# Eight rows, three projections: older rows' products placed ahead of each new row on TensorE

## The chip, the cores and the metric

The kernel runs on one core of one Trainium2 chip. The metric is the device time of one execution in microseconds (us). A core has five engines that run beside each other and wait for each other by semaphores: TensorE (in the profile PE for matmuls, PEld for the weight loads that go with them), VectorE (DVE), ScalarE (ACT), GpSimd (POOL) and SyncE (SP, which here issues most DMAs). Each engine works through its own list of instructions in a fixed order.

## The reference

The reference is a decoder trunk of two layers over 512 tokens of width 1024. The part that matters here is the entry of the first layer: the input is normalised, multiplied by a gain, and projected.

```python
def rms_norm(x, g):
    xf = x.astype(jnp.float32)
    y = xf * lax.rsqrt(jnp.mean(xf * xf, axis=-1, keepdims=True) + EPS)
    return (y * g.astype(jnp.float32)).astype(x.dtype)
...
h = rms_norm(x, ln_mix[layer])
mkv = mem_n @ w_mem_kv[layer]
...
proj = h @ w_in
...
b_logit = proj[..., o2:o2 + GDN_HEADS].astype(jnp.float32)
a_logit = proj[..., o2 + GDN_HEADS:o2 + 2 * GDN_HEADS].astype(jnp.float32)
```

`proj` holds, per token, queries, keys and values of six heads (128 wide each), a gate `z`, twelve columns of logits for the gates `a` and `b`, and queries into 256 memory tokens. `mkv` gives keys and values of these memory tokens, for both layers. After the entry come a convolution over time, the gated delta rule, an output projection, two feed-forward blocks and a second layer with sliding-window attention; the change touches none of them.

## The kernel before, in words

Everything is kept transposed: the width of 1024 lies in eight rows of 128 partitions, the 512 tokens lie along the free dimension. "Row k" below is one such slab of 128 x 512. Matmuls are done in a split form: a number is written as a high part (rounded) and a low part (the rest), and a product of two such numbers takes three matmuls, high by high, high weight by low activation, low weight by high activation. That is `mm3` (L196): three matmuls of 128 x 512, in the profile `pj<-h,whi`, `pj<-l,whi` and `pj<-h,wlo`. A weight block of 128 x 1024 is split by `weight` (L182): ScalarE copies it into `whi`, VectorE subtracts to get `wlo`. Three such pairs exist at a time, so a fourth block waits until the first is used up.

`mem_and_norm` (L294) computes the keys and values of the memory tokens for both layers, and the norm of x. For the second layer's, `values` (L371) accumulates two tiles, each 128 x 256, in two PSUM banks with the tag `pj`; ScalarE later scales them out into `kt` (L387), which frees these banks. PSUM is divided at L251: three banks with tag `pj`, two with `g`, three with `sc`. A bank is given to a new tile once the last reader of its old tile is done.

`first_rows` (L429) is the place of the change. It opens four accumulations of 128 x 512: `self.ab` (a `sc` bank), the twelve gate columns; and `begun[0]`, `begun[1]`, `begun[2]` (three `pj` banks), the first three key projections, heads 0, 1 and 2. It then loops over k. For k below eight it prepares row k: VectorE multiplies x by gain and norm (L447, `x<-x,gains,xr`), ScalarE makes the high part (L448, `h<-x`), VectorE the low part (`l<-x,h`); then come two matmuls of the gate columns (L450 and L451, `sc<-h,wabs` and `sc<-l,wabs`). At k = 1 and k = 3 the weights of the second and third projection are split. At k = 4 the tiles `kt` are evicted: `next(keys)` and `next(values)`; in `values` the copy is placed behind the ScalarE copy of row 4 by an ordering edge (`after = self.copied`, L384 and L388). Last in each turn come the products: projection 0 takes row k, projection 1 row k - 2, projection 2 row k - 5 (`trail = (0, 2, 5)`).

What order the instructions have on each engine is settled when the program is built: a planner takes, by its own estimates of time, the instruction that is ready and stands earliest in the program text. `nosync` (L116) adds an edge that fixes that one instruction stands behind another on the same engine; on the chip it costs no semaphore. The finished order on each engine is then fixed, and the engine waits at an instruction whose input, or whose bank, isn't ready.

After the loop, `gates` (L482, called at k = 8) copies `ab` out, sorts it with eight small matmuls, and computes the gates in a long chain over ScalarE, VectorE, TensorE and a DMA. `gdn` (L541) goes on: the three begun projections are convolved (`conv_tile`, L531), put through Silu and transposed, while TensorE works at the next projections.

Of the kernel before, what the change touches and what calls it, by code (L numbers as in the profile page):

```python
# [21 lines left out]
KD = D // P  # L22
# [64 lines left out]
class Builder:  # L87
# [108 lines left out]
    def mm3(self, ps, w, k, act, start, stop, more=False):  # L196

        (wh, wl), (ah, al) = w, act
        s = slice(k * P, (k + 1) * P)
        self.mm(ps, wh[:, s], ah, start, False, more)  # L200
        self.mm(ps, wh[:, s], al, False, False, more)
        self.last = self.mm(ps, wl[:, s], ah, False, stop, more)

# [225 lines left out]
    def first_rows(self, ep, x, xr, keys, values):  # L429

        nc, w = self.nc, []
        self.h = []
        self.ab = self.bank("sc")
        self.begun = [self.bank("pj") for _ in range(3)]

        def product(h, k):
            if 0 <= k < KD:
                self.mm3(self.begun[h], w[h], k, self.h[k], k == 0, k == KD - 1)


        trail = (0, 2, 5)
        w.append(self.weight(self.a["win"][H]))
        for k in range(KD + trail[-1]):
            if k < KD:
                self.h.append(self.pair(self.apool))
                xk = x[:, k, :]
                self.stt(xk, xk, self.gain(G_MIX[0], k), xr, ALU.mult, ALU.mult)  # L447
                self.split(xk, *self.h[k])  # L448
                hi, lo = self.h[k]
                self.mm(self.ab, self.wab[:, k, :], hi, k == 0, False)  # L450
                self.mm(self.ab, self.wab[:, k, :], lo, False, k == KD - 1)  # L451
                if k == 4:
                    next(keys)
                    next(values)
                if k in (1, 3):
                    w.append(self.weight(self.a["win"][H + len(w)], after=(self.copied, self.low)))
            elif k == KD:
                self.gates(ep)
            for h, n in enumerate(trail):
                product(h, k - n)  # L460

    def memory_columns(self, mr, mc, after):

# [1053 lines left out]
```

## Time and profile before

| | |
|---|---|
| median of 3 runs | 1143.69 us (1141.78, 1143.69, 1144.18) |
| the profiled execution's own time | 1142.63 us |
| its span, first to last instruction | 1140.8 us |
| TensorE busy with matmuls | 1128.5 us, 99% of the span |
| weight loads | 991.3 us, 87% |
| VectorE, ScalarE, GpSimd | 831.0, 632.0 and 86.6 us |
| mean granted TensorE clock | 0.998 of full speed |

In a timeline, a row gives the start and the duration in us, the engine, the line of the kernel (a helper's line, so L146 is every matmul and L140 nearly every ScalarE copy), the operation, the tile written and those read, the shape, how many such instructions follow each other, and, in brackets, idle time of the engine ahead of it and what ended that. Matmuls are pipelined: a row of 0.39 us starts every 0.23 us, so the time that a matmul takes is read from start to start. In a table of windows, a row gives the busy time of each engine in a stretch, with the number of instructions, then the granted clock, the share of the DMA engines and GB/s.

### The profile page before, as it was taken

To read this page: it belongs to the slowest core of one execution; us is meant where nothing else is said; L and a number is where in the kernel's file an instruction comes from. 1 tells how busy PE (TensorE), PEld (TensorE's weight loads), DVE (VectorE), ACT (ScalarE), POOL (GpSimd) and SP (SyncE) were. 2 spreads that over 40 slices of the span, in tenths; PEclk is the share of its full clock that TensorE was granted. 3 is DMA by queue.
4 is the path that set the end of the run, shared out by engine and by line. 5 is a ranking of instruction groups with operands and counts; after the bars stand their busy time and mean duration, and the time that the engine had idled before them with its cause. 6 is when DMAs were issued, how large, how long until landed. Compare 5 with 4: busy or idle time off the path is not lost. (4 is left out here: it accounts for less than half of the span.)

```text
span 1140.8 us, 19304 instructions
## 1 busy us (share of the span) xinstructions
PE 1128.5 (99%) x7337; PEld 991.3 (87%) x7337; DVE 831.0 (73%) x1543; ACT 632.0 (55%) x1267; POOL 86.6 (8%) x99
## 2 busy tenths in 40 slices
PE   9999999999999999999999999999999999999996
PEld 9888778887899988899988787788999988999886
DVE  7664976577888975588955877839989544889554
ACT  8588664566566632366643555956566322666433
POOL 0230000000111001011000000000111000111000
PEclk9999999999999999999999999999999999999999
DMA  8344242234667536378533321116677533776232
GB/s 311 117 143 148 93 130 85 84 120 148 180 148 195 140 107 175 109 169 201 128 92 98 131 73 38 56 42 199 151 190 180 141 97 104 182 187 146 85 94 86
DMA packets 72560, 151.15 MB, mean 132 GB/s; under 512 B 16860, under 2 KB 18932, under 8 KB 72468
## 3 DMA queue, kind: packets, MB, share of 16 engines
q1 hardware_dynamic: 61060, 129.21, 35.9%
q0 software_dynamic: 11136, 20.45, 11.0%
q8 instruction: 57, 0.93, 0.3%
q14 instruction: 35, 0.29, 0.1%
q10 hardware_dynamic: 272, 0.26, 0.1%
HBM read 142.94 MB, written 6.96 MB: 131 GB/s over the span
## 5 line engine op out<-in xcount | busy, mean ns | idle before, releaser
L140 ACT ACTIVATE whi<-wraw 128x512 fp32r<-128x512 f32 (+3 forms) x318 | 236.0, 749 | 248.5 <-PE pj L146 163.5
L153 DVE TENSOR_TENSOR wlo<-wraw,whi 128x512 fp32r<-128x512 f32 (+3 forms) x318 | 264.6, 842 | 94.2 <-ACT whi L140 88.6
L146 PE MATMUL pj<-h,whi 128*128 128x512 f32 (+1 forms) x652 | 256.4, 395 | 0.0
L146 PE MATMUL pj<-l,whi 128*128 128x512 f32 (+1 forms) x652 | 254.6, 391 | 0.0
L146 PE MATMUL pj<-h,wlo 128*128 128x512 f32 (+1 forms) x652 | 254.2, 390 | 0.0
L146 PE MATMUL g<-T,whi 128*128 128x256 f32 x1216 | 218.6, 280 | 0.6 <-ACT fs L140 0.6
L146 PEld LDWEIGHTS g<-T,whi 128*128 128x128 f32 x1216 | 186.0, 188 | 2.0 <-DVE fu L156 1.2
L146 PE MATMUL g<-T,wlo 128*128 128x256 f32 x608 | 170.1, 280 | 0.0
L146 PEld LDWEIGHTS pj<-h,whi 128*128 128x128 f32 x652 | 122.5, 188 | 27.5 <-issue 3.4
L146 PE MATMUL g<-h,wlo 128*128 128x256 f32 (+1 forms) x500 | 146.0, 292 | 0.0
L146 PE MATMUL g<-l,whi 128*128 128x256 f32 (+1 forms) x500 | 146.0, 292 | 0.0
L146 PE MATMUL g<-h,whi 128*128 128x256 f32 (+1 forms) x500 | 145.6, 291 | 0.0
L146 PEld LDWEIGHTS pj<-h,wlo 128*128 128x128 f32 x652 | 122.5, 188 | 25.1 <-issue 0.9
L146 PEld LDWEIGHTS pj<-l,whi 128*128 128x128 f32 x652 | 122.7, 188 | 24.4 <-issue 0.6
L146 PEld LDWEIGHTS g<-T,wlo 128*128 128x128 f32 x608 | 114.3, 188 | 0.0
L146 PEld LDWEIGHTS g<-l,whi 128*128 128x128 f32 x500 | 95.1, 190 | 2.0
L146 PEld LDWEIGHTS g<-h,wlo 128*128 128x128 f32 x500 | 95.2, 190 | 1.8
L146 PEld LDWEIGHTS g<-h,whi 128*128 128x128 f32 x500 | 95.0, 190 | 1.9
L1215 POOL DMA_DIRECT2D ws<-in_wgu x38 | 33.5, 882 | 717.5 <-DMA ws<-in_wgu 480.3
L140 ACT ACTIVATE whi<-ws 128x512 fp32r<-128x512 f32 x76 | 48.0, 632 | 48.7 <-PE g L146 40.3
L153 DVE TENSOR_TENSOR fu<-pj,rstd 128x512 f32<-128x512 f32 (+1 forms) x34 | 22.4, 659 | 54.3 <-PE pj L146 54.2
L153 DVE TENSOR_TENSOR wlo<-ws,whi 128x512 fp32r<-128x512 f32 x76 | 52.0, 685 | 7.0 <-ACT whi L140 7.0
(394 smaller groups left out, 1712.8 us busy)
## 6 DMA issues: line engine op xcount, KB each, us to landing
wraw<-in_wgu SPq DMA_DIRECT2D x50, 512.0 KB, 4.1
ws<-in_wgu SPq DMA_DIRECT2D x76, 256.0 KB, 3.4
ws<-in_wgu POOLq DMA_DIRECT2D x76, 256.0 KB, 4.6
wraw<-in_win SPq DMA_DIRECT2D x26, 512.0 KB, 3.6
wraw<-in_wdn SPq DMA_DIRECT2D x32, 384.0 KB, 3.1
wraw<-in_wdn SPq DMA_DIRECT2D x32, 320.0 KB, 2.9
wraw<-in_wgu SPq DMA_DIRECT2D x38, 256.0 KB, 4.2
wraw<-in_wout SPq DMA_DIRECT2D x16, 512.0 KB, 3.5
```

Source lines behind the costliest of these rows:

```text
L140: self.copied = self.nc.scalar.activation(out, in_, AF.Copy, **kw).ins
L146: return self.nc.tensor.matmul(out, lhsT, rhs, start=start, stop=stop, skip_group_check=more).ins
L153: return eng.tensor_tensor(out=out, in0=a, in1=b, op=op).ins
L1215: nc.gpsimd.dma_start(s1, a22, accum_op=ALU.add)
```

## The change

Three things change, all in `first_rows` and the helper `mm3`.

- In each turn of the loop the products of projection 2 (row k - 5) and projection 1 (row k - 2) are now issued ahead of the two gate matmuls of row k and of projection 0's product with row k.
- From k = 2 to k = 7 an edge places the first gate matmul of row k behind the last matmul of the product issued just before, which is projection 1's with row k - 2.
- From k = 2 to k = 7 another edge places the first matmul of projection 0's product with row k behind the second gate matmul of row k. `mm3` now keeps its first matmul in `self.head` for that.

What is computed, and the number of instructions, stays.

```diff
@@ -197,7 +197,7 @@
         (wh, wl), (ah, al) = w, act
         s = slice(k * P, (k + 1) * P)
-        self.mm(ps, wh[:, s], ah, start, False, more)
+        self.head = self.mm(ps, wh[:, s], ah, start, False, more)
         self.mm(ps, wh[:, s], al, False, False, more)
         self.last = self.mm(ps, wl[:, s], ah, False, stop, more)
@@ -446,9 +446,6 @@
                 self.split(xk, *self.h[k])
-                hi, lo = self.h[k]
-                self.mm(self.ab, self.wab[:, k, :], hi, k == 0, False)
-                self.mm(self.ab, self.wab[:, k, :], lo, False, k == KD - 1)
                 if k == 4:
                     next(keys)
                     next(values)
@@ -456,8 +453,16 @@
                     w.append(self.weight(self.a["win"][H + len(w)], after=(self.copied, self.low)))
             elif k == KD:
                 self.gates(ep)
-            for h, n in enumerate(trail):
-                product(h, k - n)
+            for h in (2, 1):
+                product(h, k - trail[h])
+            if k < KD:
+                for i, part in enumerate(self.h[k]):
+                    ins = self.mm(self.ab, self.wab[:, k, :], part, k + i == 0, k + i == KD)
+                    if k > 1 and not i:
+                        self.nosync(ins, self.last)
+            product(0, k)
+            if 1 < k < KD:
+                self.nosync(self.head, ins)
```

## The prediction

> **What bounds the kernel now.** I read the page first: its table of busy time and the chain of work that ended last.
>
> ```profile
> PE 1128.5 (99%) x7337; PEld 991.3 (87%) x7337; DVE 831.0 (73%) x1543; ACT 632.0 (55%) x1267; POOL 86.6 (8%) x99
> ...
> PE 27%; ACT 1%; DVE 0%; DMA 0%; issue 0%; DVEq 0%; ACTq 0%
> ```
>
> TensorE is busy all the time, and the recorded chain is TensorE's. No matmul is added or removed, so only TensorE's idle time can change, and what is lost or won early reaches the end unless a later wait of TensorE is for something that doesn't come from TensorE. Next the table of windows around the changed stage:
>
> ```profile
> 7.22:31.67 24.45, 24.45 (x195) 23.39 (x193) 22.31 (x40) 22.97 (x49) 0.00 (x0) 1.00 0.79 302
> 31.67:46.31 14.64, 14.05 (x62) 10.85 (x61) 10.14 (x16) 4.96 (x9) 2.35 (x4) 1.00 0.40 141
> 46.31:54.76 8.45, 8.45 (x46) 7.20 (x44) 4.17 (x10) 4.64 (x10) 2.32 (x4) 1.00 0.21 66
> 54.76:100.00 45.24, 45.24 (x236) 37.93 (x235) 30.20 (x55) 41.50 (x120) 12.13 (x8) 1.00 0.40 122
> ```
>
> The first columns are the stretch, its length and TensorE's busy time: 0.59 us is missing in 31.67 to 46.31 us and nothing behind it. The timeline of TensorE shows where, and in which order the rows come:
>
> ```profile
> 31.79 0.40 PE L146 MATMUL sc<-h,wabs 128*128 128x512 f32 x1
> ...
> 33.87 0.40 PE L146 MATMUL pj<-h,wlo 128*128 128x512 f32 x1
> 34.10 0.40 PE L146 MATMUL sc<-h,wabs 128*128 128x512 f32 x1
> ...
> 35.51 0.40 PE L146 MATMUL pj<-h,whi 128*128 128x512 f32 x1
> 36.19 0.50 PE L146 MATMUL sc<-l,wabs 128*128 128x512 f32 x1 [0.28 <-DVE l L153]
> 36.52 0.40 PE L146 MATMUL pj<-l,whi 128*128 128x512 f32 x1
> ...
> 37.22 0.40 PE L146 MATMUL pj<-h,whi 128*128 128x512 f32 x1
> 37.92 0.50 PE L146 MATMUL sc<-l,wabs 128*128 128x512 f32 x1 [0.31 <-DVE l L153]
> 38.26 0.39 PE L146 MATMUL pj<-l,whi 128*128 128x512 f32 x1
> ...
> 38.96 0.39 PE L146 MATMUL pj<-h,whi 128*128 128x512 f32 x1
> ```
>
> From 31.79 to 34.10 us ten matmuls start: gate columns and projection 0 of rows 0 and 1, 0.231 us each. Rows 2, 3 and 4 follow the same way, and TensorE stands still twice, before the low part of rows 3 and 4. Start to start, 35.51 to 36.19 is 0.68 and 37.22 to 37.92 is 0.70, against 0.23; the matmul after each wait starts 0.33 later instead of 0.23. That is 0.45 + 0.47 + 0.10 + 0.11 = 1.13 us. Whole triples (h, l, wlo) of an older row first appear at 38.96; until then TensorE has nothing of projections 1 and 2.
>
> **Why it has nothing of them.** This decides the case. The banks with tag pj are three. The ScalarE and VectorE timelines show who frees them:
>
> ```profile
> 24.10 0.75 DVE L153 TENSOR_TENSOR m<-pj,mr 128x256 f32<-128x256 f32 x2
> ```
>
> ```profile
> 27.41 0.48 ACT L140 ACTIVATE m<-pj,mc 128x256 f32<-128x256 f32 x1
> ```
>
> ```profile
> 35.72 1.14 ACT L140 ACTIVATE h<-x 128x512 fp32r<-128x512 f32 x2
> 36.77 0.81 ACT L140 ACTIVATE kt<-pj,mc 128x256 f32<-128x256 f32 x2
> ```
>
> ```profile
> 36.77 0.45 ACT L140 ACTIVATE kt<-pj,mc 128x256 f32<-128x256 f32 x1
> ```
>
> Two banks come free at 24.10 to 24.85 and are taken by the second layer's memory values; the third comes free at 27.89 and becomes projection 0's. The banks of projections 1 and 2 are those of the memory values, and they come free only with the two kt copies on ScalarE: the first ends at 36.77 + 0.45 = 37.22, the second at 36.77 + 0.81 = 37.58. Those copies are tied behind row 4's high part (rows 4 and 5 are the pair at 35.72), and nothing in the change moves them.
>
> **The change part by part.**
>
> (1) Gate columns and projection 0 of row 2 move behind projection 1's product with row 0, by an edge. Rows 0 and 1 run as before to 34.10. Then TensorE stands at that product until its bank is free. The weights aren't what it waits for; VectorE's timeline has them, and the rows:
>
> ```profile
> 31.72 1.22 DVE L153 TENSOR_TENSOR wlo<-wraw,whi 128x1024 fp32r<-128x1024 f32 x1
> ...
> 35.45 0.68 DVE L153 TENSOR_TENSOR l<-x,h 128x512 fp32r<-128x512 f32 x1
> 36.05 1.22 DVE L153 TENSOR_TENSOR wlo<-wraw,whi 128x1024 fp32r<-128x1024 f32 x1
> 37.19 0.68 DVE L153 TENSOR_TENSOR l<-x,h 128x512 fp32r<-128x512 f32 x1
> ...
> 40.49 1.35 DVE L153 TENSOR_TENSOR l<-x,h 128x512 fp32r<-128x512 f32 x2
> ```
>
> The second projection's low weights end at 32.94. After 35.45 + 0.68 = 36.13 the waiting matmul starts at 36.19, so a release costs 0.06. The product starts at 37.22 + 0.06 = 37.28: idle 37.28 - 34.10 = 3.18, plus 0.10 for the slow restart, 3.28 us. Behind it in TensorE's queue stand all later rows, and the edges let none of them pass; before, rows 2 and 3 ran in that time. Bounds: if the planner puts the kt copy ahead of row 5's copy, it ends about one such copy (1.14 / 2 = 0.57) earlier: 2.71. If the product gets the other bank, 37.58: 3.64. I take 3.28, the order and the bank of before, because nothing ahead of those copies depends on what is moved.
>
> (2) The two old stalls go: -1.13 us. Rows 3 and 4 then come 8 and 16 matmuls after 37.28, at about 39.9 and 41.7 for their gate columns, and their low parts are ready at 36.13 and 37.87. The later rows are ready by 40.49 + 1.35 = 41.84 and are needed from there on one each 2.5 us; the third projection's weights end at 37.27 and its bank at 37.58. What is late next is nothing in this stage.
>
> (3) The moved gate columns feed the gates. Behind the new start stand 54 matmuls up to the last of them (12 of gate columns, 18 of projection 1, 15 of projection 0, 9 of projection 2): 37.28 + 0.10 + 54 x 0.230 = 49.80. In before ScalarE's chain behind them was this, and two later rows of TensorE are:
>
> ```profile
> 46.50 0.60 ACT L140 ACTIVATE ab<-sc 128x512 f32<-128x512 f32 x1 [5.38 <-PE sc L146]
> 47.02 1.06 ACT L140 ACTIVATE whi<-wraw 128x1024 fp32r<-128x1024 f32 x1
> ...
> 51.32 1.06 ACT L140 ACTIVATE whi<-wraw 128x1024 fp32r<-128x1024 f32 x1 [0.64 <-PE pj L146]
> ...
> 55.34 1.84 ACT L140 ACTIVATE kn<-pj,gains 128x512 f32<-128x512 f32 x3
> ...
> 59.65 0.64 ACT L134 ACTIVATE kn<-kn 128x512 f32<-128x512 f32 x1 [1.51 <-DVE kn L156]
> ```
>
> ```profile
> 54.76 0.39 PE L146 MATMUL sc<-h,whi 128*128 128x512 f32 x1
> ```
>
> ```profile
> 61.66 0.42 PEld L150 LDWEIGHTS g<-consts,kn 128*128 128x128 f32 x4 [0.37 <-ACT kn L134]
> ```
>
> The copy of ab, which started at 46.50, starts at about 50.0; so it is 3.5 us later, while TensorE is 3.28 - 1.13 = 2.15 later. Copies, table load, convolutions and Silu hang behind it, and the weight split at 51.32 (freed by projection 1's last product) moves by some 2.6. So ScalarE's chain falls 0.4 (2.6 - 2.15) to 1.3 us (3.5 - 2.15) behind TensorE. TensorE's next wait on it is the transposes at 61.66. If they keep their place, TensorE pays up to 1.3; but some twenty matmuls of the fifth key projection stand beside them, and the planner can put them first: 0. I take 0.25, nearer to nothing, since the last window above shows TensorE without idle time while ScalarE is 92% busy (41.50 of 45.24).
>
> (4) Other queues. SP's weight loads, the gates' DMA and POOL's additions behind it move by the same 3.5 us or less. Weights for the fourth key projection: high part after projection 0's last product, 50.5 instead of 47.02, low part some 2.3 us later, at 52.8, needed at 54.76 + 2.15 = 56.9. Hidden by 4 us; without that cover it would cost whatever passes 56.9. The edges cost nothing themselves: same engine, no semaphore.
>
> Sum: 3.28 - 1.13 + 0.25 = +2.40 us. The profiled execution took 1142.63 (span 1140.8 and 1.8 around it), so 1145.0 by it; its time is 1.06 below the median 1143.69, and on the median the forecast is 1146.1, 0.21% slower. From no change, about 0.2% (2.3 us) can be told.
>
> **The rivals.**
>
> A, not slower: projection 1's bank isn't what TensorE waits for, the product runs at 34.10, and both stalls go: -1.13, 1142.6. For it: in before the planner may have held projection 1 back for its weights, not for the bank. Against it: three banks, two held to 37.22 and 37.58, and no older product before 38.96. It decides from where the first kt copy ends before 34.1 + 1.1 = 35.2; row 4's copy, which it must follow, starts at 35.72. Chance 0.10.
>
> B: the kt copy comes ahead of row 5's: 2.71 - 1.13 + 0.25 = +1.8, 1145.5. For it: the text has kt before row 5. Against: the planner chose otherwise from the same inputs. Chance 0.08.
>
> C: the long stall drops the TensorE clock. The windows at the end of before show such a drop, and TensorE's timeline the start:
>
> ```profile
> 1133.60:1137.00 3.40, 0.00 (x0) 0.00 (x0) 2.07 (x4) 0.75 (x2) 1.27 (x1) 1.00 0.42 137
> 1137.10:1140.80 3.70, 0.00 (x0) 0.00 (x0) 0.00 (x0) 0.00 (x0) 0.00 (x0) 0.50 0.45 148
> ```
>
> ```profile
> 1.19 3.57 PE L146 MATMUL g<-wabs 128*128 128x256 f32 x15 [1.19 <-DVE eps L288]
> ...
> 7.26 0.28 PE L146 MATMUL pj<-mh,wlo 128*128 128x256 f32 x1
> 7.38 0.28 PE L146 MATMUL pj<-whi,mh 128*128 128x256 f32 x1
> ```
>
> ```profile
> 1132.77 0.70 PE L146 MATMUL g<-fg,ones 128*128 128x256 f32 x2 [0.99 <-ACT fg L143]
> ```
>
> The last matmul ends at 1133.47; the granted clock is still 1.00 to 1137.0 and then 0.50, so some 3.5 us without a matmul halve it. The first 15 matmuls took 3.57 / 15 = 0.238 us each, those at 7.26 to 7.38 take 0.12: half rate from 1.19 to about 7.2, some 6.0 us, which cost 3.0. The new stall of 3.18 is just under 3.5, less what the last matmul before it still runs. If it did drop the clock, the price is between half of 3.5 (an equal time to come back, my estimate) and 3.0: +1.8 to 3.0, so 1147.9 to 1149.1. It decides from a stall of 3.5 us. For it: only 0.3 us are left, and the rows quoted of before have nothing between a 0.70 us step and this end. Against: 3.18 has not reached the 3.5 that the one drop in the trace took. Chance 0.10. The Trainium skill, page TensorE: Matmul & The Clock Gate, section "HAM oscillation — how this bites in real kernels", states the rule that TensorE must not idle for more than about 3.4 us, or it runs at half rate for a while; the section before says that the windows run free of the kernel. By that rule the stall stays just inside and the sum is unchanged; the drop 3.5 us after the last matmul agrees with it, and no row of before shows what a window does that is mostly idle.
>
> **How the numbers follow.** The likeliest case holds 0.72: 1146.1, and its own range is 1145.4 (no cost in part 3, and the spread of the runs) to 1147.3 (part 3 at 1.3, or the other bank). A lies below at 1142.6, B inside, C above. The range that leaves out A and the upper part of C, widened by the spread of the three runs, is 1143.6 to 1148.6. Slower by over 0.2%: a good half of the likeliest case, since its 2.40 lies just past the 2.3 that can be told, and all of C: 0.54. Within: the rest of it, B, most of A: 0.41. Faster: A with a gain further on: 0.05.
>
> **What would show it.** In the profile after: no wait for a low part of rows 3 and 4; one idle stretch of about 3.2 us ahead of the first `pj<-h,whi` after row 1's triple, ended by ScalarE's kt at about 37.2; ab copied near 50 us; the fourth key projection at about 56.9 instead of 54.76; the kt copies still behind row 5's. Wrong would make it: products of projection 1 at 34.1 (A), kt ahead of row 5 (B), a granted clock below 1 after the stall (C), or a planner that, seeing other times, puts later work in another order: I give that no term, since the windows behind 46 us are full.

## The result, and the profile after

The changed kernel took 1150.49 us (median of 7 runs, 1148.91 to 1153.03), the kernel before, on the same chip, 1144.18 (7 runs, 1141.78 to 1147.64): a ratio of 1.0052 [1.0035, 1.0068], some 6 us slower. The forecast was +2.40 us, so its range was left on the slow side. The profiled execution took 1150.49 us, 7.86 more than that of before, and its span is 1148.4 against 1140.8.

The page of the changed kernel, its busy times:

```profile
PE 1131.4 (99%) x7337; PEld 992.6 (86%) x7337; DVE 829.8 (72%) x1543; ACT 633.0 (55%) x1267; POOL 85.6 (7%) x99
```

The page alone hides the loss: TensorE's share is still 99%, and the count of matmuls is the same. Its 2.9 us of additional busy time are a first hint that matmuls ran slower. The table of windows, by the same stretches as before, has both parts.

```profile
31.67:46.31 14.64, 11.70 (x39) 9.03 (x38) 9.88 (x15) 4.75 (x9) 2.36 (x4) 0.77 0.40 137
...
54.76:100.00 45.24, 42.74 (x210) 34.81 (x208) 25.50 (x41) 37.36 (x110) 13.53 (x10) 1.00 0.41 129
```

In the first stretch TensorE is idle for 2.94 us (0.59 before) and its granted clock is 0.77 (1.00 before). In the last one it is idle for 2.50 us where there was nothing. The waits of TensorE between 24 and 110 us (total, times, longest) name what ended them:

```profile
PE pj L146 <- ACT kt L140: 2.9, 1, 2.9
PE pj L146 <- DVE kn L156: 2.5, 1, 2.5
```

TensorE's timeline shows the places:

```profile
33.66 0.40 PE L146 MATMUL pj<-h,wlo 128*128 128x512 f32 x1
37.01 0.80 PE L146 MATMUL pj<-h,whi 128*128 128x512 f32 x1 [2.94 <-ACT kt L140]
...
43.10 0.40 PE L146 MATMUL pj<-l,whi 128*128 128x512 f32 x1
...
58.77 0.39 PE L146 MATMUL sc<-h,whi 128*128 128x512 f32 x1
...
59.63 0.46 PE L146 MATMUL g<-consts,gate 128*128 128x128 f32 x2
...
67.82 0.47 PE L146 MATMUL pj<-h,whi 128*128 128x512 f32 x1 [2.49 <-DVE kn L156]
```

Three things cost time.

First, the wait for the bank. From 33.66 to 37.01 are 3.35 us from start to start, 0.23 of which is the usual pitch: 3.12 lost, with the release by `kt` that was forecast. The two waits for low parts (1.13) are gone: +1.99.

Second, the clock. From 37.01 to 43.10 fourteen matmuls start, 6.09 us for what takes 14 x 0.23 = 3.22 at full rate: +2.87.

Third, a wait of 2.5 us at 67.82: the fifth key projection wants a `pj` bank, and the convolution of the first head on VectorE (L156) has not yet read it. In before TensorE did not wait there.

Together 1.99 + 2.87 + 2.49 = 7.35 of the 7.6 by which the span grew. The fourth key projection starts only 4.01 us late (58.77 against 54.76) and not 4.86. The stage began 0.21 us earlier (33.66 against 33.87), and six small matmuls of the gates, which ran ahead of it in before and took 0.59 us there (51.58 to 52.17), now come behind it: the first of them is at 59.63 above, and in before it was here:

```profile
51.58 0.39 PE L146 MATMUL g<-consts,gate 128*128 128x128 f32 x2
```

ScalarE's timeline tells why the convolution is late:

```profile
35.46 1.13 ACT L140 ACTIVATE h<-x 128x512 fp32r<-128x512 f32 x2
36.50 0.82 ACT L140 ACTIVATE kt<-pj,mc 128x256 f32<-128x256 f32 x2
...
52.55 0.60 ACT L140 ACTIVATE ab<-sc 128x512 f32<-128x512 f32 x1 [11.69 <-PE sc L146]
...
56.76 1.06 ACT L140 ACTIVATE whi<-wraw 128x1024 fp32r<-128x1024 f32 x1 [0.76 <-PE pj L146]
57.72 0.32 ACT L134 ACTIVATE l<-l,ones 128x48 f32<-128x48 f32 x1
59.16 1.06 ACT L140 ACTIVATE whi<-wraw 128x1024 fp32r<-128x1024 f32 x1 [1.11 <-DMA wraw<-in_win]
60.48 0.27 ACT L140 ACTIVATE row<-g 24x128 f32<-24x128 f32 x1 [0.27 <-PE g L146]
...
63.18 1.85 ACT L140 ACTIVATE kn<-pj,gains 128x512 f32<-128x512 f32 x3
```

And of before, two rows of the same timeline that the prediction doesn't show:

```profile
50.34 0.33 ACT L134 ACTIVATE l<-l,ones 128x48 f32<-128x48 f32 x1
52.36 0.27 ACT L140 ACTIVATE row<-g 24x128 f32<-24x128 f32 x1
```

In before the gates' logarithm (`l<-l,ones`) came first, at 50.34, then the weight split for the fifth projection (51.32), then the gates' copy of `row` (52.36), and the split for the sixth much later. In the changed kernel the planner has put the fifth split (56.76) ahead of the logarithm and the sixth (59.16), which waits 1.11 us for its DMA, ahead of `row`. So the chain of the gates, 6.05 us late at `ab` (52.55 against 46.50), is 8.12 us late at `row` (60.48 against 52.36), while TensorE is late by 4.86. The copies that begin the convolutions stand behind it on ScalarE: 63.18 against 55.34, 7.84 us late.

The clock itself shows in windows of the length in which it changes:

```profile
32.80:36.21 3.41, 1.26 (x6) 0.69 (x4) 3.41 (x6) 2.23 (x4) 0.00 (x0) 1.00 0.53 174
36.21:39.62 3.41, 2.62 (x6) 2.13 (x7) 3.41 (x7) 1.16 (x4) 1.36 (x3) 0.50 0.46 142
39.62:43.04 3.42, 3.42 (x9) 2.65 (x9) 1.93 (x3) 1.21 (x2) 1.00 (x2) 0.50 0.46 165
43.04:46.45 3.41, 3.41 (x16) 2.76 (x16) 0.00 (x0) 0.00 (x0) 0.00 (x0) 1.00 0.00 0
```

TensorE was busy for 1.26 us of the window up to 36.21, 37% of it, and right behind it the clock is half. It stays half through a window that is busy for 77% and through one that is busy throughout, and is full again at 43.04.

### The profile page after: what moved, and what is told of

Its sections match the earlier page's. It is cut to its first block, busy times and chain, and to the rows that moved or that the text cites. A ratio compares the mean times of both kernels' runs of the same rounds, so it can differ in the third digit from the quotient of the medians.

```text
span 1148.4 us, 19306 instructions
## 1 busy us (share of the span) xinstructions
PE 1131.4 (99%) x7337; PEld 992.6 (86%) x7337; DVE 829.8 (72%) x1543; ACT 633.0 (55%) x1267; POOL 85.6 (7%) x99
```

## The experiments

In outline, the theory after the result had two parts: one wait (for the bank of `kt`) that also halves the clock, and a second wait that comes from the new order of the gates' work and not from the first. The rival was that everything is one cause: the late bank makes all later work late, and the rest follows. All differences below are medians against the kernel before on the same chip (1142.54 to 1143.07 us).

**The changed kernel once more.**

> The changed kernel once more, unchanged, beside kernels of the same chip. Some 6 us above the kernel before. The clock windows lie at random against the program, so the stretch at half clock behind the 3 us stall may last one window (3.4 us) or two (6.8 us) or be missing, and the runs should spread by about 3 us.

Measured: 1149.94 us, 1.0060 [1.0048, 1.0073], +6.87 us; the five runs lie within 1.6 us, less than the 3 that were expected. The windows, at the first wait and at the second:

```profile
34.47:37.88 3.41, 0.62 (x3) 0.53 (x4) 3.41 (x6) 3.10 (x6) 0.00 (x0) 1.00 0.35 129
37.88:41.30 3.42, 3.42 (x10) 2.65 (x9) 3.38 (x7) 1.26 (x2) 2.35 (x4) 0.50 0.79 250
65.19:68.60 3.41, 1.74 (x11) 1.56 (x12) 3.41 (x6) 2.43 (x4) 1.75 (x2) 1.00 1.00 305
```

The clock falls again at the first wait, now for one window of 3.41 us instead of two, because the windows lie elsewhere against the work. At the second wait the window is busy for 51% and the clock stays full.

**The bank freed early.** In the changed kernel the copies of `kt` for the values are issued at k = 2, so that their bank is free before projection 1 needs it.

```diff
+                if k == 2:
+                    next(values)
                 if k == 4:
                     next(keys)
-                    next(values)
```

> The changed kernel, with the memory values' copies kt taken at k = 2 instead of k = 4 (the keys stay at k = 4), so that the banks of projections 1 and 2 come free near 33 us. Theory 1 (the bank holds TensorE at 33.9 us, and that stall drops the clock and delays the gates): no wait for kt, no stretch at half clock, the fourth key projection (first matmul on the sc bank) at about 53.7 us instead of 58.8, no wait for the convolution's bank near 65 us; 1 us below the kernel before, 7 us below the changed kernel. Theory 2 (the order alone makes the gates late, whatever the bank does): the wait near 65 us stays with 2 to 3 us, and the time is 1 to 2 us above the kernel before. Theory 3 (the clock fell by chance, not by the stall): half clock can show here too, near 36 to 43 us.

Measured: 1145.13 us, 1.0025 [1.0014, 1.0036], +2.25 us. The waits of TensorE, ScalarE's timeline and the windows:

```profile
PE pj L146 <- DVE kn L156: 2.5, 1, 2.5
```

```profile
46.83 0.60 ACT L140 ACTIVATE ab<-sc 128x512 f32<-128x512 f32 x1 [5.78 <-PE sc L146]
...
53.27 1.06 ACT L140 ACTIVATE whi<-wraw 128x1024 fp32r<-128x1024 f32 x1 [0.95 <-PE pj L146]
54.76 0.27 ACT L140 ACTIVATE row<-g 24x128 f32<-24x128 f32 x1 [0.44 <-PE g L146]
```

```profile
60.07:63.48 3.41, 1.38 (x8) 1.23 (x9) 3.41 (x6) 2.48 (x4) 1.77 (x2) 1.00 0.99 310
63.48:66.89 3.41, 3.41 (x11) 2.86 (x11) 3.41 (x6) 3.31 (x17) 3.41 (x4) 0.50 0.22 81
```

The price, a little above the 1 to 2 us expected for a second wait alone, includes a drop of the clock. The first wait and the two old ones are gone, and `ab` is copied at 46.83, only 0.33 later than before. Yet `row` comes 2.40 later (54.76 against 52.36), behind the same two weight splits, and the second wait is there in full. So it does not come from the first. In this profile it dropped the clock, behind a window that is busy for 40%.

**The same in the kernel before.** Is the early bank worth anything by itself?

> The kernel before, with nothing but the copies kt at k = 2 instead of k = 4. Theory 1 (the banks alone kept projections 1 and 2 back in before): the planner can now place older products of projection 1 ahead of row 3 by itself, the two waits for a low part (1.1 us together) shrink or go, and the time is up to 1 us below the kernel before. If it was the planner's estimate of the weights that kept them back, the order on TensorE stays and so does the time, within 0.3 us.

Measured: 1141.68 us, 0.9993 [0.9984, 1.0002]. TensorE's waits between 24 and 110 us are gone, the low parts' included, and the fourth key projection starts at 53.90 instead of 54.76. A second measurement:

> The kernel before with the kt copies at k = 2, once more. The two low-part waits are gone (1.1 us): 0.5 to 1 us below the kernel before.

Measured: 1142.17 us, 0.9996 [0.9987, 1.0005]. Neither differs from before by more than its interval. In the two profiles the gain is not lost at once: most of it goes in a late wait of TensorE for VectorE's `sqa`, near 1122 us, which takes 1.53 and 1.76 us here and 0.47 in before. The run without both new waits, further on, shows its rows.

**Work put into the first wait.** Twelve matmuls whose result is not used stand between row 1 and projection 1's first product, so that TensorE is not idle; the bank comes as late as before.

```diff
+            if k == 2:
+                ins, ps = self.last, self.bank("g")
+                for i in range(12):
+                    after, ins = ins, self.mm(ps, self.ones_r, self.h[0][0], i == 0, i == 12 - 1)
+                    self.nosync(ins, after)
             for h in (2, 1):
                 product(h, k - trail[h])
+                if k == 2 and h == 1:
+                    self.nosync(self.head, ins)
```

> The changed kernel, with twelve matmuls of 128 x 512 into a spare bank (ones times row 0, result not used) put by edges between row 1 and projection 1's first product, 2.8 us of work in the 3.0 us in which TensorE waits for kt. The wait for the bank stays, the product still starts near 37.0 us. Theory 1 (the stall drops the clock): the clock stays at full, the matmuls behind come each 0.23 us, not 0.43, and the time is about 3 us below the changed kernel. Theory 3 (the drop has nothing to do with the stall): half clock stays, and the time is that of the changed kernel.

Measured: 1149.07 us, 1.0056 [1.0044, 1.0068], +6.19 us. TensorE's timeline:

```profile
34.12 2.96 PE L146 MATMUL g<-h,ones 128*128 128x512 f32 x12
37.22 0.50 PE L146 MATMUL pj<-h,whi 128*128 128x512 f32 x1
...
65.27 0.47 PE L146 MATMUL pj<-h,whi 128*128 128x512 f32 x1 [2.48 <-DVE kn L156]
```

and of ScalarE's:

```profile
50.00 0.60 ACT L140 ACTIVATE ab<-sc 128x512 f32<-128x512 f32 x1 [8.93 <-PE sc L146]
```

The clock stays at full rate here, projection 1 starts at 37.22 as it must, `ab` is copied at 50.00, which is the time that the prediction gave, and the second wait stays. By the spans the kernel gains 2.0 us on the changed one (1146.4 against 1148.4), but by the medians only 0.1 to 0.7 (+6.19 against +6.31 and +6.87). That is a miss in size: if the clock is the only difference, the medians should show it too. The traces show a part of the answer. A matmul well behind both waits, `g<-m,qm`, starts at 123.01 us here and at 125.53 and 124.60 in the two profiles of the changed kernel, so 1.6 to 2.5 us are won up to there; but at 303.36 TensorE then waits 0.97 us for a weight split, a wait that neither kernel has. The next runs take the second wait away, to see the first one alone.

**The second wait taken away.** In the changed kernel the fifth key projection goes to an `sc` bank, which does not depend on the convolution.

```diff
-                               self.project(a["win"][H + h], self.h, "sc") if h == 3 else None)
+                               self.project(a["win"][H + h], self.h, "sc") if h in (3, 4) else None)
```

> The changed kernel, with the fifth key projection accumulated in an sc bank instead of a pj bank, which the convolution of the first head has to free. First stall and half clock stay (37.0 us, 36 to 43 us). If the second wait of TensorE (2.5 us near 65 us, released by the convolution) is for that bank: it goes, and the time is 2 to 3 us below the changed kernel. If the gates' late chain holds TensorE in another way too (transposes, weights), the wait moves to them, and the gain is under 1 us.

Measured: 1147.34 us, 1.0041 [1.0029, 1.0053], +4.46 us. The only wait of TensorE left between 24 and 110 us is the one for `kt`, 2.9 us. The windows:

```profile
34.09:37.50 3.41, 0.51 (x3) 0.32 (x3) 3.41 (x5) 3.34 (x6) 0.00 (x0) 1.00 0.39 137
37.50:40.91 3.41, 3.41 (x10) 2.64 (x9) 3.38 (x7) 1.18 (x2) 2.35 (x4) 0.50 0.72 223
```

The second wait is gone and nothing takes its place. 6.87 - 4.46 = 2.41 us were its price: the wait, and what the clock may add to it in some executions. With the first measurement of the changed kernel, +6.31, it is 1.85. Each of these medians has an interval of some 1.4 us to either side, so that the second figure behind the point means little.

The five executions of this run also show what the clock costs within one kernel. Their mean granted clocks are 0.994, 0.994, 0.995, 0.996 and 0.998, and their times 1147.53, 1147.34, 1148.34, 1146.61 and 1145.30 us. The one at 0.998, which before has too, is 1.3 to 3.0 us faster than the others.

**The first wait alone.** The fifth projection on an `sc` bank, and the twelve matmuls of the run above: a wait for the bank with neither the clock nor the second wait.

> The changed kernel, with twelve filler matmuls in the stall for kt, and the fifth key projection in an sc bank: the first stall stays, the half clock and the second wait are taken away. The first stall alone is left: 3.1 us less the 1.1 us of the two old waits, 2 us above the kernel before, and no half clock between 24 and 1100 us.

Measured: 1145.33 us, 1.0021 [1.0012, 1.0029], +2.26 us. TensorE's timeline:

```profile
37.58 0.50 PE L146 MATMUL pj<-h,whi 128*128 128x512 f32 x1
```

This is near what the prediction's first two terms give together, +2.15. That it is so close has some luck in it: the wait for a weight split near 300 us is here too, 0.98 us. And 4.46 - 2.26 = 2.20 us is what the half clock costs; the one execution above without a drop lies 2.42 us above before (1145.30 - 1142.88), near the 2.26 here.

**Six matmuls instead of twelve**, to ask how much idle time the clock bears.

> The changed kernel with six filler matmuls instead of twelve in the stall for kt, and the fifth key projection in an sc bank: TensorE is idle for about 1.6 us instead of 3. If the clock falls only where most of a window is idle: no half clock, the same 2 to 3 us above the kernel before as with twelve fillers. If any idle time near 1.5 us is enough: half clock for one or two windows behind 37 us in some runs, and 1.7 to 3 us more.

Measured: 1145.24 us, 1.0023 [1.0014, 1.0032], +2.70 us. Waits, then windows:

```profile
PE pj L146 <- ACT kt L140: 1.9, 1, 1.9
```

```profile
34.38:37.79 3.41, 1.53 (x7) 0.90 (x5) 3.41 (x6) 3.02 (x6) 0.00 (x0) 1.00 0.49 154
37.79:41.20 3.41, 3.40 (x15) 2.78 (x16) 3.37 (x8) 1.13 (x3) 2.15 (x4) 1.00 0.61 204
```

The window with the wait is busy for 1.53 of 3.41 us, 45%, and the clock does not fall. The price is that of the twelve, within their intervals: as long as the clock stays up, what the wait costs doesn't depend on whether TensorE is idle in it.

**A longer first wait.** The copies of `kt` at k = 6 instead of 4, and the fifth projection on an `sc` bank.

```diff
-                if k == 4:
+                if k == 6:
                     next(keys)
                     next(values)
```

> The changed kernel with the kt copies at k = 6, which stand on ScalarE behind row 7's copy, and the fifth key projection in an sc bank. If the bank held by kt is the whole of the first stall, it ends with the first kt copy again, now near 41.6 us: 4.8 us later than in the changed kernel. The clock is then at half from inside the stall, for one window or two behind it. With 2.3 us from the first stall without half clock, 4.8 more, and up to 2.9 for the clock: 7 to 10 us above the kernel before.

Measured: 1151.05 us, 1.0071 [1.0059, 1.0084], +8.51 us. TensorE's timeline and the windows:

```profile
40.87 0.79 PE L146 MATMUL pj<-h,whi 128*128 128x512 f32 x1 [6.48 <-ACT kt L140]
```

```profile
34.58:37.99 3.41, 0.00 (x0) 0.00 (x0) 3.41 (x6) 2.27 (x4) 0.00 (x0) 1.00 0.33 127
37.99:41.41 3.42, 0.54 (x1) 0.50 (x2) 3.39 (x7) 1.99 (x4) 0.24 (x1) 0.50 0.47 153
41.41:44.82 3.41, 3.41 (x9) 2.64 (x8) 0.37 (x1) 0.00 (x0) 2.12 (x4) 0.50 0.44 154
```

The product follows its bank to 40.87, and within the intervals each microsecond of the wait is paid: the bank comes 40.87 - 37.01 = 3.86 later than in the changed kernel, and this run costs 8.51 - 4.46 = 4.05 more than the one with the copies at k = 4. The half clock lasts 6.83 us, through a window that is busy for 16% and one that is busy throughout.

**Both waits taken away.** The changed kernel with the `kt` copies at k = 2 and the fifth projection on an `sc` bank:

> The changed kernel, with the kt copies at k = 2 and the fifth key projection in an sc bank: both banks that TensorE waited for are taken away. If the two waits, with the half clock behind them, are all that the change costs: no wait of TensorE over 1 us between 24 and 110 us, and 1 us below the kernel before (the two low-part waits are gone). If the late gates hold it elsewhere (transposes): up to 2 us above that.

Measured: 1142.81 us, 1.0001 [0.9988, 1.0014], -0.26 us. TensorE has no wait between 24 and 110 us. The two banks account for the loss. The 1 us below before that was expected is not there, though, and the end of the traces shows where it went. These are TensorE's rows, first of before, then of this run:

```profile
1122.34 0.70 PE L146 MATMUL g<-sqa,ones 128*128 128x256 f32 x2 [0.47 <-DVE sqa L153]
```

```profile
1122.32 0.70 PE L146 MATMUL g<-sqa,ones 128*128 128x256 f32 x2 [1.79 <-DVE sqa L153]
```

The matmul ahead of it starts 1.34 us earlier in this run (1120.25 against 1121.59), this one at the same time: what is won early is lost in front of it. VectorE's `sqa` needs a tile of ScalarE, which works without a gap from 1115.45 us up to it, and what ScalarE waits for at 1115.45 is the DMA of a weight block; in before this wait ends at 1115.46.

**The gates put ahead of the weight splits.** The same early `kt`, but the fifth projection stays on its `pj` bank; edges place the splits of the fifth and sixth weights behind the gates' `row` copy on ScalarE and behind the gates' last product on VectorE.

```diff
-        self.stt(g, g, -1.0, ea.unsqueeze(2).to_broadcast([P, H, NC]), ALU.mult, ALU.mult)
+        self.gated = self.stt(g, g, -1.0, ea.unsqueeze(2).to_broadcast([P, H, NC]), ALU.mult, ALU.mult)
...
         self.copy(row, pg[:NH, 64:64 + P])
+        self.rowed = self.copied
...
-                               self.project(a["win"][H + h], self.h, "sc") if h == 3 else None)
+                               self.project(a["win"][H + h], self.h, "sc") if h == 3 else self.project(
+                                   None, self.h, w=self.weight(a["win"][H + h], after=(self.rowed, self.gated))))
```

> The changed kernel, with the kt copies at k = 2, and by two edges the weight splits of the fifth and sixth key projection behind the gates' row copy on ScalarE and the gates' last product on VectorE; the fifth stays in a pj bank. If the second wait came from the place that the planner gave these splits ahead of the gates: the row copy comes at about 52 us instead of 54.8, the wait for the convolution's bank (2.5 us near 62 us) goes, and the time is 1 us below the kernel before. If the gates are late for another reason, the wait stays, and the time is 3 us above.

Measured: 1142.84 us, 1.0000 [0.9991, 1.0009], -0.23 us. Waits, then ScalarE's timeline:

```profile
PE pj L146 <- DVE kn L156: 0.7, 1, 0.7
```

```profile
47.15 0.60 ACT L140 ACTIVATE ab<-sc 128x512 f32<-128x512 f32 x1 [5.77 <-PE sc L146]
...
53.03 0.27 ACT L140 ACTIVATE row<-g 24x128 f32<-24x128 f32 x1 [2.07 <-PE g L146]
53.20 1.04 ACT L140 ACTIVATE whi<-wraw 128x1024 fp32r<-128x1024 f32 x1
```

With `ab` even a little later than in the first of these runs (47.15 against 46.83), `row` comes 1.73 earlier, and the second wait shrinks from 2.5 to 0.7 us. So the order of the splits against the gates made most of it: 1.8 of 2.5 us, in the kernel with the early `kt`.

**The text without the edges.** The changed order of the program text, but neither of the two `nosync` edges:

```diff
                     ins = self.mm(self.ab, self.wab[:, k, :], part, k + i == 0, k + i == KD)
-                    if k > 1 and not i:
-                        self.nosync(ins, self.last)
             product(0, k)
-            if 1 < k < KD:
-                self.nosync(self.head, ins)
```

> The changed kernel without its two edges: the products of projections 2 and 1 only stand earlier in the program text. The planner's order then has rows 2 to 4 as before, ahead of projection 1, so no wait for kt and no half clock near 37 us, and the two low-part waits of before (1.1 us) stay. On ScalarE the splits of the fifth and sixth projection stand ahead of the gates' row copy as in the changed kernel. If it is this order that makes the second wait: TensorE waits 2.5 us for the convolution's bank near 63 us, and the time is 2 to 4 us above the kernel before. If the second wait needs the edges, the time is that of the kernel before within 0.5 us.

Measured: 1147.16 us, 1.0041 [1.0029, 1.0054], +4.62 us. Waits, then windows:

```profile
PE pj L146 <- DVE kn L156: 2.5, 1, 2.5
PE sc L146 <- DVE l L153: 0.7, 2, 0.4
```

```profile
61.28:64.69 3.41, 1.41 (x8) 1.27 (x9) 3.41 (x6) 2.47 (x5) 1.12 (x1) 1.00 0.97 315
64.69:68.10 3.41, 3.41 (x11) 2.85 (x11) 3.41 (x6) 3.35 (x17) 3.41 (x4) 0.50 0.23 85
```

No wait for `kt` here, and the two for low parts are back: the first stage is again much as before. The second wait is there all the same, and it drops the clock behind a window that is busy for 41%. So the move of the text alone brings the second wait, and the edges the first. The price is above the 2 to 4 us expected, and the clock is hardly the reason: the other four executions have a mean clock of 0.997 or 0.998, as before has, and took 1147.02 to 1148.14 us. Some 1.2 us of it are the late wait for `sqa`, 1.68 us at 1127.42 against 0.47; the rest is not accounted for.

## Why the prediction was wrong, point by point

Two steps failed, worth 2.2 and 2.4 us by medians: the decision point of rival C, which kept the price of the clock out of the sum, and, in term 3, the place where TensorE next waits for ScalarE's chain, with no term for another order of the planner.

**Term 1, the wait for the bank (+3.28): right.** 3.12 in the profile, ended by `kt`, with the copies still behind row 5's (36.50, after rows 4 and 5 at 35.46). Rivals A and B fall: nothing of projection 1 ran at 34.10, and the copy did not pass row 5's.

**Term 2, the two old waits (-1.13): right in the profile,** where neither is left. Terms 1 and 2 together, +2.15, were measured as +2.26 in the run that has the first wait alone. The gain by itself is not to be seen at the end: with the two old waits and the two new ones gone the median is 0.26 us below before, and that is within the interval. In the profile it goes in the late wait for `sqa`.

**Rival C is what happened on top.** The clock did fall, for a price of 2.87 in the profile and 2.20 between medians; the price that the prediction gave, 1.8 to 3.0, holds for both, though the one window of the second profile costs less (some 1.6 us, worked out in the last section). Wrong was its decision point, "a stall of 3.5 us", and so its chance of 0.10. It was read from the only drop in the trace, an end without any matmul, which can't tell a whole idle window from a mostly idle one. The runs show that a window of 3.41 us with some work in it suffices: in the stages of this change, busy for 0, 15, 18, 37, 40 and 41% it drops, for 45 and 51% it doesn't. A wait of 2.94 us makes such a window in most positions, not in all: cut in half by an edge, it leaves two windows that are each busy for 57%. Of the five executions with the fifth projection on an `sc` bank, one shows no sign of a drop. The rule of the Trainium skill that the prediction cited (page TensorE: Matmul & The Clock Gate, section "HAM oscillation — how this bites in real kernels"), no idle time over about 3.4 us, is too weak here: the wait of 2.94 us, and those of 2.5 us in two runs, halved the clock. The measurement decides.

**Term 3, ScalarE's chain (+0.25, at most 1.3): the place was wrong, and the size.** The direction was right: the gates fall behind TensorE. `ab` would have been copied near 50.0 (it was, in the run with twelve matmuls), and the rest of its delay, to 52.55, comes from the clock. But the step "TensorE's next wait on it is the transposes at 61.66" failed. What TensorE waits for is a bank: the fifth key projection takes that of the first, which the convolution must have read. It measured 2.4 us (2.41 between medians, or 1.85 from the first measurement; 2.49 in the profile). And the term "a planner that puts later work in another order: I give that no term, since the windows behind 46 us are full" failed: full windows on TensorE say that there is work to be done, not that its banks will be free when the order of other engines changes. The planner put two weight splits ahead of the gates; the run with the two edges shows that this order makes most of the wait, and the one without edges that the move of the text is enough to bring it.

**Term 4, other queues (0): right as far as it went.** The fourth projection's weights hid no wait. The DMA of the sixth projection's weights, which ScalarE waited 1.11 us for ahead of `row`, was not thought of.

By medians the loss of 6.87 us is so 2.26 for the first wait with the old ones gone, 2.20 for the clock and 2.41 for the second wait. These are steps between runs, one taken after the other, so their sum is no check; the check is that the first profile, one execution with two windows at half clock, gives 1.99, 2.87 and 2.49 for the same three, and that without both waits nothing is left. The late waits near 300 and 1122 us, up to 1.8 us, differ between these kernels and blur all such differences.

**What stays open.** Why twelve matmuls in the first wait moved the medians by less than 1 us while the second wait is present, and by 2.2 without it: a drop of the clock at the second wait in some executions, as in two other runs, can be only a part of it, since the two executions with a mean clock of 0.998 and 0.999 still took 1148.46 and 1147.58 us. The wait near 300 us is another part, but the run without the second wait has it too. What in the planner's estimates moves the splits ahead of the gates. And whether the kernel before would gain from the early `kt` copies if the weights near 1115 us came sooner.

## What to carry to other kernels

When work is moved ahead on a busy engine, ask for each product not only whether its inputs are there but who has to free its bank, and look for the queue on which that reader stands: here two such banks, read by ScalarE and VectorE, cost some 2.3 and 2.4 us. A planner that orders by ready time and text is part of the change: compare the order of all engines behind the place, since a move of text without any edge cost 0.41%. A gain early in the kernel can be lost far behind it: here 1.3 us of one went at a late wait whose chain hangs on a DMA that came no earlier. A wait of two to three microseconds on TensorE can cost well over its length, because the clock may go down behind it; six matmuls put into such a wait kept the clock up.

## What the runs showed of the hardware

The granted clock of TensorE changes in steps of one window of 3.41 us, and the windows lie differently against the work in each execution (36.21 in one profile of the changed kernel, 37.88 in the other). What counts is how busy the window before was: in the stages of this change the next one had half the clock after a window busy for 41% or less, and full clock after one busy for 45% or more. But the share of busy time is not the exact measure. Near the end of the run without both waits there is a window busy for 46%, with matmuls of 128 x 256, and behind it, at 1134.29, the clock is half:

```profile
1130.87:1134.29 3.42, 1.59 (x8) 0.78 (x7) 1.17 (x3) 1.22 (x3) 0.00 (x0) 1.00 0.00 0
```

A row of such a matmul lasts 0.28 us and the next starts 0.12 later, so the busy time may overstate the work there; what the clock goes by was not measured.

The way back needs more: after windows busy for 77% and for 16% the clock stayed half, after those that were busy throughout it was full. So the same wait costs one window at half rate in one execution and two in the next. At half rate a matmul of 128 x 512 starts every 0.43 us (39.73 to 40.16 in the first profile of the changed kernel) instead of every 0.23. A window busy throughout so loses 3.41 x (1 - 0.23 / 0.43) = 1.6 us, an estimate; over the two windows of that profile, the first of them partly idle, it was 2.87 us.
